# A one-core encoder layer: operands of the MLP's first product made early, parked in device memory and loaded at the borders of token chunks; gate weights split by columns

## The chip, the cores and the metric

The kernel runs on one core of a Trainium2 chip. The metric is the device time of one execution in microseconds (us); for the kernel before it is 1885.21 us, the median of three runs (1883.59 to 1886.38).

## What is computed

One encoder layer over two token groups with shared weights, 512 and 1024 tokens of width 1024, all in float32. Cut to what matters here:

```
h = x + concat(attention, pooling) @ w_out          # attention stage
m = rmsnorm(h, norm_mlp_g)
h = h + square(relu(m @ w_up)) @ w_down             # MLP: 1024 -> 4096 -> 1024
gate = sigmoid(rmsnorm(h, norm_ple_g) @ w_ple_gate)
h = h + gate * (p @ w_ple_proj)                     # gate stage
y = rmsnorm(h, final_norm_g)
```

Every matrix operand is kept as a sum of two parts, a rounded high part and the rest as a low part, and a product takes three matmuls (high by high, high by low, low by high).

## The kernel before

**Tiling.** The 1536 tokens are three chunks c of 512 (`CH`). An activation tile is 128 features by 2 blocks of 128 features by 512 tokens: four of them, `hT[c][a]`, make up a chunk's residual `h`. All tiles of any size share one pool of 49 equal slots of on-chip memory (line 76); a load waits until the slot that it was given is released.

**Order of the work.** Four engines (TensorE, ScalarE, VectorE, GpSimd) follow the order in which the program writes their instructions (line 72); the transfers are all issued by SyncE's one queue. `load` (line 55) keeps a load's place in that order behind the last matmul written before it, without a wait on it. Small work that is to be slipped in between is a generator in the list `chores`; `step()` (line 519) advances the first one by one step. In the attention loop `step` is called once in an iteration `at` (some of them only, lines 1046 to 1047), and in the MLP once after every product.

**Attention stage** (to about 580 us): when a chunk's `h` is finished (`heads_out`, line 735), two chores are queued: `mean_square` (line 641), which squares `h`, sums the squares by features on GpSimd, sums over the partitions by a matmul with ones and stores the row in `w_d[c]`, and `spill` (line 700), which stores `h` in device memory.

**MLP stage** (580 to 1683 us): 48 *pairs* of hidden blocks, 16 for each chunk (class `Pair`, line 756). The first product of a pair is done with seven block products instead of eight. Its token operands, `MO[c][i]` for i = 1 to 7, are made by `operands(c)` (line 599) from four copies `m` of the chunk's `h` (`load_m`, line 594): 8 scalings by `norm_mlp_g` (ScalarE), 8 differences (VectorE), 14 high parts (ScalarE) and 14 low parts (GpSimd and VectorE in turn); each operand is two slots of 128 x 4 x 256. The weights' side is made by `feed` (line 774), some four products ahead.

`run` (line 831) writes a pair in this order, where P means one of the seven products (12 matmuls of 256 columns) and D(a) the second product of the pair before, for one tile of `h` (`down`, 12 matmuls of 512 columns): P1, D(0), P6, P2, D(1), P5, P7, D(2), P3, P4, D(3). `after(i)` comes behind each product and holds the weights' feed, a quarter of the split of the second product's weights, in a chunk's last pair the steps of the next chunk's `operands`, and a `step()`. P3 goes on in the PSUM bank of P5 and waits until VectorE has made `u4` of it (line 858); D(0) waits for the two `r` (line 878).

The MLP runs on unscaled `h`: at a chunk's first pair (g = 0) `raise_h(c)` (line 661) multiplies the four tiles of `h` by the stored row (VectorE), and after the chunk the row is inverted (`invert`, line 667) and multiplied in (`lower_h`), and `stat_g` gets the gate's norm; these are chores of the next chunk's pairs, and for the last chunk of the gate stage. Their loads (`load_h`, `load_ms`) are written at the top of the pair.

*Border 1* is the change from attention to the MLP: the last pieces of `fill`, then `operands(0)` and the mean squares as chores, four steps of the weights' feed, then pair 0 (lines 1060 to 1070; pair 0 has no D). *Borders 2 and 3* are the changes of chunk at pairs 16 and 32. *Border 4* is the change to the gate stage (lines 1171 to 1182): the weights of the two gate products are loaded by rows (`load_g`, `load_p`), scaled by `norm_ple_g` and split (`split_g`), and `gate_in` makes the token operands of chunk 0; all of this is queued before the last four D and stepped through there.

**Gate stage** (from 1683 us): `gate` (line 1187) does one block of 128 output features: `pj`, 6 matmuls, then `pg`, 24 matmuls over the eight row blocks k of the gate weights.

## Time and profile before

| what | value |
|---|---|
| median of three runs | 1885.21 us (1883.59 to 1886.38) |
| the profiled execution: its own time / its span | 1887.41 us / 1885.6 us |
| mean granted TensorE clock, share of full speed | 0.970 |
| TensorE busy | 1772.4 us, 94% of the span |
| weight loads / VectorE / ScalarE / GpSimd busy | 82% / 66% / 50% / 54% |
| moved by DMA | 203.60 MB, 31.1% of the DMA engines' time |

Times in the rows are microseconds from the start of the span. PE is TensorE's matmuls, DVE VectorE, ACT ScalarE, POOL GpSimd, SPq SyncE's queue. A row of a timeline gives the start, the duration, the engine, the line, the operation with output and inputs, how many were joined into the row, and in brackets the idle time ahead of it with what ended it. Line 49 is the helper through which every matmul goes, so PE rows are told apart by their tiles: px, py, pz and pq are the banks of the first product (px: P1 and P2, py: P6, pz: P5 and P3, pq: P7 and P4), pd is the second product, w the ones-matmul of a mean square, pj and pg the gate's.

### The profile page before, as it was taken

What the parts mean: (1) busy time and instruction counts of PE and PEld (TensorE: products, weight loads), DVE (VectorE), ACT (ScalarE), POOL (GpSimd) and SP (SyncE); (2) the same over time, 40 slices, a digit from 0 to 9 for tenths busy, and PEclk for the clock granted to TensorE, in tenths of its full rate; (3) what the DMA queues carried; (4) which work ended last, traced back from release to release, by engine and by line L of the source; (5) the groups of instructions that cost most, each with busy time, mean ns of one, the idle gap of its engine ahead of it and who ended that gap; (6) DMA issues with size and microseconds to landing.
All of it is one profiled execution on the core that took longest, in us unless ns stands there. A gap on an engine that the chain in (4) does not pass through costs nothing.

```text
span 1885.6 us, 28256 instructions
## 1 busy us (share of the span) xinstructions
PE 1772.4 (94%) x10540; PEld 1552.4 (82%) x10540; DVE 1246.7 (66%) x1829; ACT 937.7 (50%) x1830; POOL 1013.9 (54%) x888
## 2 busy tenths in 40 slices
PE   9999899999994799999969999998899999979997
PEld 7888777988873789989958899987788899968897
DVE  5677856888874656555587855556786655573765
ACT  6344456677864444454545544455455444451332
POOL 4475765455545565566556665565556665561122
PEclk9999999999996899999979999999899999999998
DMA  6333453010212433232433423242333332240102
GB/s 238 112 135 146 173 205 135 24 57 29 90 73 99 158 101 101 90 109 95 133 109 119 142 90 112 90 136 87 125 134 105 105 104 90 93 165 12 62 34 101
DMA packets 59929, 203.60 MB, mean 108 GB/s; under 512 B 7568, under 2 KB 10000, under 8 KB 59792
## 3 DMA queue, kind: packets, MB, share of 16 engines
q1 hardware_dynamic: 59792, 201.80, 31.1%
q8 instruction: 83, 1.36, 0.3%
q14 instruction: 54, 0.44, 0.1%
HBM read 169.53 MB, written 32.24 MB: 107 GB/s over the span
## 4 chain that ended last, share of the span: by engine, by line
PE 56%; DVE 5%; ACT 2%; issue 2%; POOL 1%; DMA 0%; POOLq 0%; DVEq 0%; SPq 0%; ACTq 0%
PE pd L49 26%; PE pz L49 7%; PE pq L49 7%; PE px L49 6%; PE pg L49 5%; PE py L49 3%; PE pj L49 1%; DVE h L1241 1%; DVE r L878 1%; DVE wg L1085 1%; DVE h L829 1%; DVE wd L809 0%; DVE mo L626 0%; DMA w<-w_d 0%; DVE h L675 0%
## 5 line engine op out<-in xcount | busy, mean ns | idle before, releaser
L49 PE MATMUL pd<-r,wd 128*128 128x512 f32 x2304 | 571.8, 397 | 19.3 <-DVE r L878 19.3
L49 PEld LDWEIGHTS pd<-r,wd 128*128 128x128 f32 x2304 | 422.7, 190 | 108.0 <-DVE r L878 23.9
L779 POOL TENSOR_TENSOR w<-ws,w 128x512 fp32r<-128x512 f32 x192 | 273.7, 1430 | 235.3 <-ACT w L778 226.4
L829 DVE TENSOR_TENSOR h<-pd,h 128x1024 f32<-128x1024 f32 x192 | 234.4, 1221 | 112.1 <-PE pd L49 112.1
L779 POOL TENSOR_TENSOR w<-wur,w 128x512 fp32r<-128x512 f32 x144 | 212.3, 1487 | 177.0 <-ACT w L778 175.3
L778 ACT CAST w<-ws 128x512 fp32r<-128x512 f32 x192 | 118.6, 618 | 245.4 <-DVE ws L787 214.3
L461 POOL TENSOR_SCALAR pr<-pr,rr 128x512 f32<-128x512 f32 x160 | 111.1, 705 | 145.0 <-DVE rr L456 73.2
L49 PEld LDWEIGHTS pz<-mo,w 128*128 128x128 f32 x1152 | 153.3, 193 | 30.2 <-issue 22.0
L49 PE MATMUL pz<-mo,w 128*128 128x256 f32 x1152 | 156.5, 286 | 21.0 <-DVE u L858 21.0
L49 PE MATMUL z<-w,x 128*128 128x512 f32 (+1 forms) x864 | 175.1, 359 | 1.2 <-DVE w L160 0.5
L49 PEld LDWEIGHTS z<-w,x 128*128 128x128 f32 x864 | 142.4, 188 | 28.2 <-ACT w L159 2.1
L809 DVE TENSOR_TENSOR wd<-wdr,wd 128x512 fp32r<-128x512 f32 x96 | 99.5, 1036 | 98.1 <-ACT wd L808 91.7
L49 PE MATMUL pq<-mo,w 128*128 128x256 f32 x1152 | 155.4, 285 | 1.8 <-DVE c L862 1.6
L49 PE MATMUL px<-mo,w 128*128 128x256 f32 x1152 | 153.5, 283 | 0.0
L49 PE MATMUL pg<-hg,wg 128*128 128x512 f32 (+1 forms) x768 | 142.6, 341 | 11.1 <-DVE h L829 11.1
L49 PEld LDWEIGHTS px<-mo,w 128*128 128x128 f32 x1152 | 148.1, 191 | 4.2
L49 PEld LDWEIGHTS pq<-mo,w 128*128 128x128 f32 x1152 | 146.2, 193 | 2.6 <-issue 2.5
L49 PEld LDWEIGHTS pg<-hg,wg 128*128 128x128 f32 x768 | 120.7, 191 | 28.9 <-issue 11.5
L472 ACT CAST pt<-tp 128x512 fp32r<-128x512 f32 x160 | 87.9, 592 | 91.9 <-PE tp L53 90.1
L809 POOL TENSOR_TENSOR wd<-wdr,wd 128x512 fp32r<-128x512 f32 x96 | 127.2, 1325 | 6.0 <-ACT wd L808 6.0
L473 DVE TENSOR_TENSOR pt<-tp,pt 128x512 fp32r<-128x512 f32 x160 | 104.1, 684 | 33.1 <-ACT pt L472 32.9
L878 DVE TENSOR_TENSOR r<-c,r 128x512 fp32r<-128x512 f32 x96 | 77.7, 815 | 70.1 <-ACT c L875 56.1
(192 smaller groups left out, 2979.5 us busy)
## 6 DMA issues: line engine op xcount, KB each, us to landing
wur<-in_w_up_dram SPq DMA_DIRECT2D x96, 512.0 KB, 3.8
wdr<-in_w_down_dram SPq DMA_DIRECT2D x96, 512.0 KB, 3.7
h_d<-h SPq DMA_DIRECT2D x16, 512.0 KB, 2.8
h<-h_d SPq DMA_DIRECT2D x16, 512.0 KB, 5.8
xn<-in_xn_dram SPq DMA_DIRECT2D x12, 512.0 KB, 6.2
qs_d<-qs SPq DMA_DIRECT2D x12, 512.0 KB, 3.0
yT_d<-y SPq DMA_DIRECT2D x12, 512.0 KB, 2.9
qb<-qs_d SPq DMA_DIRECT2D x12, 512.0 KB, 4.3
```

The source lines that it names most:

```text
L49: last_pe[0] = nc.tensor.matmul(*a, **k).ins
L461: gp.tensor_scalar(p, p, rr, 1.0, op0=ALU.mult, op1=ALU.mult)
L472: sc.copy(self.pt[kt][:, 0], tp)
L473: ve.tensor_tensor(self.pt[kt][:, 1], tp, as32(self.pt[kt][:, 0]), op=ALU.subtract)
L778: sc.copy(t[:, 0], x)
L779: gp.tensor_tensor(t[:, 1], x, as32(t[:, 0]), op=ALU.subtract)
L809: (gp, ve)[i].tensor_tensor(lo, self.dr[i][:, h], as32(hi), op=ALU.subtract)
L829: ve.tensor_tensor(h, pd.rearrange("p (a b) -> p a b", a=2), h, op=ALU.add)
L878: ve.tensor_tensor(self.r[i][:, 1], x, as32(self.r[i][:, 0]), op=ALU.subtract)
L1085: ve.scalar_tensor_tensor(WG[k][1], raw, g, as32(WG[k][0]), op0=ALU.mult, op1=ALU.subtract)
L1241: ve.scalar_tensor_tensor(h, h, gfin_sb[:, 2 * a + e:2 * a + e + 1], r, op0=ALU.mult, op1=ALU.mult)
```

## The change

- `mean_square`, `load_m` and `operands` are replaced by one chore, `make_m(c, et, el)`. For each half b of the blocks it loads two tiles of the stored `h`, squares them and adds the squares, scales them, forms the four differences on engine `et` and the seven operands' halves, the high part on ScalarE and the low part on engine `el`, and stores each half operand in device memory (`mo_d`); at the end comes the mean-square row. For chunk 0 it is queued in the attention stage with GpSimd for both engines, and there the operands are loaded back at once (`load_mo`). For chunks 1 and 2 it is queued at pair g = 1 of the chunk before, with VectorE and GpSimd, and `load_mo(c + 1, i)` is written behind product i of the chunk's last pair. The attention loop steps the chores in every iteration above 54.
- `raise_h` is no longer a chore: one tile follows each product of the chunk's first pair except product 6. The loop that emptied the chores at g = 0 is gone. `invert(c)` is done in the chunk itself at g = 1 and the inverse is stored.
- At border 1 the feed's four steps go between the last pieces of `fill`, and nothing else is run before pair 0 but the steps that these pieces take along.
- Gate weights are loaded in pieces of 512 rows by 256 columns and split by output block d, two blocks ahead of their use, without the scaling. `gate_in` now scales by `norm_ple_g`; for chunk 0 it is done during chunk 1 (`put_in`), stored, and loaded in the last pair; for chunks 1 and 2 it is done in the last block of the chunk before. The first weights (`first_weights`) are loaded and split from the last pair on.
- In `rsqrt_rows` the PSUM bank `bc` is taken later.

```diff
@@ rsqrt_rows: bc taken behind dg and the wait @@
-        bc = tp_ps(f"bc{name}")
...
+            bc = tp_ps(f"bc{name}")
...
+        bc = tp_ps(f"bc{name}")
@@ load_m, operands and mean_square go; make_m and load_mo come @@
-    def load_m(c):
...
-    def operands(c):
...
-    def mean_square(c, e=ve):
...
+    def make_m(c, et, el):
         A, B = slice(0, HF), slice(HF, CH)
+        acc = slot([P, 2, CH], F32, f"sqm{c}")
+        def squares_of(b, m):
+            for i in range(2):
+                sq = slot([P, 2, CH], F32, f"sqm{c}{b}{i}")
+                for h in range(2):
+                    out = sq[:, h] if b + i + h else acc[:, 0]
+                    yield ((lambda i=i, h=h, out=out: sc.activation(out, m[i][:, h], AF.Square)),
+                           (lambda out=out, first=b + i + h == 0: None if first else
+                            et.tensor_tensor(acc[:, 0], acc[:, 0], out, op=ALU.add)))
+        for b in range(2):
+            m = [slot([P, 2, CH], F32, f"m{c}_{2 * i + b}") for i in range(2)]
+            for i in range(2):
+                load(m[i], h_d[c][2 * i + b])
+            yield
+            yield from lagged(squares_of(b, m))
+            for i in range(2):
+                for h in range(2):
+                    k = 2 * (2 * i + b) + h
+                    sc.activation(m[i][:, h], m[i][:, h], AF.Copy, scale=gmlp_sb[:, k:k + 1])
+                yield
+            tt = [slot([P, 2, 2, HF], F32, f"t{c}_{b}{i}") for i in range(2)]
+            t1, t2, t3, t4 = (tt[i // 2][:, i % 2] for i in range(4))
+            b11, b12, b21, b22 = m[0][:, :, A], m[0][:, :, B], m[1][:, :, A], m[1][:, :, B]
+            for o, x, y in ((t1, b12, b11), (t2, b22, t1), (t3, b22, b12), (t4, b21, t2)):
+                et.tensor_tensor(o, x, y, op=ALU.subtract)
+                yield
+            def pairs():
+                for i, x in ((1, b11), (6, t2), (2, b21), (5, t1), (7, t3), (3, b22), (4, t4)):
+                    out = slot([P, 2, 2, HF], F32R, f"mm{c}_{i}{b}")
+                    def low_part(i=i, x=x, out=out):
+                        el.tensor_tensor(out[:, 1], x, as32(out[:, 0]), op=ALU.subtract)
+                        for j in range(2):
+                            sy.dma_start(mo_d[c][i][j][:, 2 * b:2 * b + 2], as32(out[:, j]))
+                        if c == 0 and b:
+                            load_mo(0, i)
+                    yield (lambda x=x, out=out: sc.copy(out[:, 0], x)), low_part
+            yield from lagged(pairs())
         sh = slot([P, 2, CH], F32R, f"sh{c}")
         sc.copy(sh[:, 0], acc[:, 0])
+        el.tensor_tensor(sh[:, 1], acc[:, 0], as32(sh[:, 0]), op=ALU.subtract)
+        yield from wait(2)
         bc = tp_ps(f"w{c}")
         for i in range(2):
             pe.matmul(bc, ones_sb, sh[:, i], start=i == 0, stop=i == 1)
+        ve.tensor_scalar(acc[:, 1], bc, 1.0 / D, EPS, op0=ALU.mult, op1=ALU.add)
+        sy.dma_start(w_d[c], acc[:, 1])
+    def load_mo(c, i):
+        MO[c, i] = [slot([P, 4, HF], F32R, f"mo{c}_{i}{j}") for j in range(2)]
+        for j in range(2):
+            load(as32(MO[c, i][j]), mo_d[c][i][j])
@@ invert @@
             ve.reciprocal(w, w)
             yield
+        sy.dma_start(w_d[c], ws[c])
@@ heads_out, a chunk's last piece @@
-                    chores.extend((mean_square(c, gp), spill(c)))
+                    chores.append(spill(c))
+                    if c == 0:
+                        chores.append(make_m(0, gp, gp))
@@ the attention loop @@
-        if at == 96:
-            load_m(0)
-        if at == 97:
+        if at == 94:
...
-            if took or at < 84 and at % 2:
+            if took or at > 54 or at % 2:
@@ border 1 @@
-    made = operands(0)
-    made = [act for i in (0, 1, 6, 2, 5, 7, 3, 4) for act in made[i]]
-    chores.append(steps_of(*[lambda i=i: [act() for act in made[i:i + 2]] for i in range(0, len(made), 2)]))
     while fill:
         fill.popleft()()
         step(2)
-    for _ in range(4):
-        next(feeding)
-        step(2)
-    while chores:
-        step()
+        if len(fill) % 2 == 0 and len(fill) < 8:
+            next(feeding)
@@ gate weights and operands @@
-    def load_g(k):
...
-    def split_g(k):
...
+    def load_g(q, j):
+        WG["r", q, j] = slot([P, 4, 2 * P], F32, f"wgr{q}{j}")
+        load(WG["r", q, j], w_gate[j * CH:(j + 1) * CH, q * 2 * P:(q + 1) * 2 * P].rearrange("(k p) d -> p k d", p=P))
+    def split_g(d, e):
+        if d not in WG:
+            WG[d] = [slot([P, KD, P], F32R, f"wg{d}_{i}") for i in range(2)]
+        for j in range(2):
+            raw = WG["r", d // 2, j][:, :, d % 2 * P:(d % 2 + 1) * P]
+            hi, lo = (x[:, 4 * j:4 * j + 4] for x in WG[d])
+            sc.copy(hi, raw)
+            yield
+            e.tensor_tensor(lo, raw, as32(hi), op=ALU.subtract)
+            yield
...
-    def gate_in(c, e, n=4):
...
+    def gate_in(c, a):
+        hl = [slot([P, 2, CH], F32R, f"hg{c}{a}_{i}") for i in range(2)]
+        for h in range(2):
+            g = gple_sb[:, 2 * a + h:2 * a + h + 1]
+            sc.activation(hl[0][:, h], hT[c][a][:, h], AF.Copy, scale=g)
+            ve.scalar_tensor_tensor(hl[1][:, h], hT[c][a][:, h], g, as32(hl[0][:, h]), op0=ALU.mult, op1=ALU.subtract)
+        gin[c, a] = hl
...
+    def put_in(c):
+        for a in range(4):
+            gate_in(c, a)
+            for i in range(2):
+                sy.dma_start(hg_d[a][i], flat(gin[c, a][i]))
+            del gin[c, a]
+            yield
+    hg_d = [[dram.tile([P, D], F32, name=f"hg_d{a}{i}") for i in range(2)] for a in range(4)]
+    def load_in(c, a):
+        gin[c, a] = [slot([P, 2, CH], F32R, f"hg{c}{a}_{i}") for i in range(2)]
+        for i in range(2):
+            load(flat(gin[c, a][i]), hg_d[a][i])
+    def first_weights():
+        for j in range(2):
+            load_g(0, j)
+        load_p(0), load_p(1), load_pp(0)
+        yield
+        for d in range(2):
+            yield from split_g(d, (gp, ve)[d])
+        split_p(0)
+        yield
+        split_p(1)
+        yield
+        split_pp(0, ve)
@@ the pairs @@
+        raising = None
         if g == 0:
             for a in range(4):
                 load_h(c, a, h_d[c][a])
             load_ms(c)
-            chores.append(raise_h(c))
-        if g == 1 and c:
-            load_ms(c - 1)
-        if g == NG - 1 and c < 2:
-            made = operands(c + 1)
-        if g == NG - 2 and c < 2:
-            load_m(c + 1)
-        if pair is last_pair:
-            load_p(0), load_p(1), load_g(0)
-            for a in range(4):
-                load_h(0, a, hl_d[0][a])
-        elif n == 0:
+            raising = raise_h(c)
+        if g == 1:
+            chores.append(invert(c))
+            if c:
+                load_ms(c - 1)
+                chores.extend((lower_h(c - 1, ve), stat_g(c - 1, ve), store_h(c - 1)))
+            if c == 1:
+                chores.append(put_in(0))
+            if c < 2:
+                chores.append(make_m(c + 1, ve, gp))
+        if n == 0:
             pair.load_down()
         splits = pair.split_down()
...
         def after(i):
             next(feeding, None)
             next(splits, None)
-            if i == 1:
-                for act in made.get(0, ()):
-                    act()
-            for act in made.get(i, ()):
-                act()
+            if raising and i != 6:
+                next(raising, None)
+            if g == NG - 1 and c < 2:
+                load_mo(c + 1, i)
+            if n == len(pairs) - 1:
+                if i == 1:
+                    chores.append(first_weights())
+                if i in (5, 7, 3, 4):
+                    load_in(0, (5, 7, 3, 4).index(i))
             step()
         pair.run(between, after)
         for _ in splits:
             pass
-        if g == 0:
-            while chores:
-                step()
-        if g == 1 and c:
-            chores.extend((invert(c - 1), lower_h(c - 1, ve), stat_g(c - 1, ve), store_h(c - 1)))
+        for _ in raising or ():
+            pass
         before = pair
-    chores.append(steps_of(lambda: split_p(0), lambda: split_p(1), lambda: split_g(0)))
-    for k in range(1, KD):
-        load_g(k)
-    load_pp(0)
-    late = gate_in(0, gp)
-    chores.append(steps_of(*[lambda: next(late) for _ in range(5)], *[lambda k=k: split_g(k) for k in range(1, KD)]))
+    for a in range(4):
+        load_h(0, a, hl_d[0][a])
     for a in range(4):
         before.down(a)
-        step(4)
+        step(2)
@@ gate @@
+        if c == 0 and d % 2 == 0 and d < KD - 2:
+            for j in range(2):
+                load_g(d // 2 + 1, j)
+        splits = split_g(d + 2, (gp, ve)[d % 2]) if c == 0 and d < KD - 2 else iter(())
         for k in range(KD):
-            ws = [x[:, cols] for x in WG[k]]
-            for i, (w_, x_) in enumerate(three(ws, [x[:, k % 2, tok] for x in gin[c, "h"][k // 2]])):
+            ws = [x[:, k, :] for x in WG[d]]
+            for i, (w_, x_) in enumerate(three(ws, [x[:, k % 2, tok] for x in gin[c, k // 2]])):
                 pe.matmul(pg, w_, x_, start=k == 0 and i == 0, stop=k == KD - 1 and i == 2)
             if k in hooks:
                 step()
+            if k % 2 == 0:
+                next(splits, None)
+            elif c < 2 and d == KD - 1:
+                del gin[c, k // 2]
+                gate_in(c + 1, k // 2)
@@ the groups of the gate stage @@
+            if c == 0 and d == 0:
+                load_ms(2)
+                chores.extend((lower_h(2, ve), stat_g(2, ve)))
             if d == 4 and c < 2:
                 load_pp(c + 1)
-                coming.append(gate_in(c + 1, ve))
+            if c == 0 and d == 4:
+                for a in range(4):
+                    load_h(1, a, hl_d[1][a])
+            if c < 2 and d == KD - 1:
+                split_pp(c + 1, ve)
             gate(c, o, w, d, sq)
-            if c == 1 and d in (5, 6):
-                next(coming[-1])
-        if c == 0:
-            load_ms(2)
-            for a in range(4):
-                load_h(1, a, hl_d[1][a])
-            chores.extend((invert(2), lower_h(2, ve), stat_g(2, ve)))
         chores.append(finish(c, o, w, sq))
     while chores:
         step()
```

## Rows read from the trace of the kernel before

**Rows 1.** Which engine is busy when: from the page, TensorE's busy share and its granted clock in 40 equal slices of 47.1 us, in tenths.

```profile
PE   9999899999994799999969999998899999979997
...
PEclk9999999999996899999979999999899999999998
```

**Rows 2.** TensorE's waits over the whole span: tile and line that waited, what ended the wait; us in total, times, longest us.

```profile
PE w L49 <- ACT sh L647: 26.3, 1, 26.3
PE pz L49 <- DVE u L858: 21.0, 3, 8.1
PE pd L49 <- DVE r L878: 19.3, 5, 8.8
PE pg L49 <- DVE h L829: 11.1, 1, 11.1
```

**Rows 3.** TensorE's timeline at border 1.

```profile
577.93 1.69 PE L49 MATMUL po<-cat,wo 128*128 128x256 f32 x12 [0.28 <-DVE h L749]
...
607.82 2.76 PE L49 MATMUL px<-mo,w 128*128 128x256 f32 x12
...
625.20 2.90 PE L49 MATMUL pz<-mo,w 128*128 128x256 f32 x12 [8.05 <-DVE u L858]
...
654.99 1.58 PE L49 MATMUL px<-mo,w 128*128 128x256 f32 x12
```

**Rows 4.** TensorE's timeline at border 2: P1 of pair 15, the wait in D(0) of pair 16, P1 of pair 17.

```profile
929.26 1.57 PE L49 MATMUL px<-mo,w 128*128 128x256 f32 x12
...
969.78 5.08 PE L49 MATMUL pd<-r,wd 128*128 128x512 f32 x11 [8.02 <-DVE r L878]
...
991.61 1.57 PE L49 MATMUL px<-mo,w 128*128 128x256 f32 x12
```

**Rows 5.** TensorE's timeline at border 3: P1 of pair 31, P1 and the D(0) behind it of pair 33, P1 of pair 34.

```profile
1289.18 1.57 PE L49 MATMUL px<-mo,w 128*128 128x256 f32 x12
...
1352.46 1.59 PE L49 MATMUL px<-mo,w 128*128 128x256 f32 x12
1353.89 3.04 PE L49 MATMUL pd<-r,wd 128*128 128x512 f32 x12
...
1373.64 1.58 PE L49 MATMUL px<-mo,w 128*128 128x256 f32 x12
```

**Rows 6.** TensorE's timeline in the gate stage: pj of the first two blocks, and of two blocks in the steady part.

```profile
1683.03 1.57 PE L49 MATMUL pj<-pp,wpj 128*128 128x512 f32 x6
...
1703.91 1.31 PE L49 MATMUL pj<-pp,wpj 128*128 128x512 f32 x5
...
1710.82 1.56 PE L49 MATMUL pj<-pp,wpj 128*128 128x512 f32 x6
...
1717.76 1.56 PE L49 MATMUL pj<-pp,wpj 128*128 128x512 f32 x6
```

**Rows 7.** SyncE's timeline at border 1: the store of the last chunk's h, then the loads of pair 0.

```profile
573.20 11.87 SPq L702 DMA_DIRECT2D h_d<-h  x4
...
609.20 1.35 SPq L56 DMA_DIRECT2D h<-h_d  x3
610.64 0.38 SPq L56 DMA_DIRECT2D w<-w_d  x1
611.08 2.45 SPq L56 DMA_DIRECT2D wdr<-in_w_down_dram  x4
```

**Rows 8.** VectorE's timeline in pair 0: the first multiplication of h, and u4.

```profile
616.93 1.22 DVE L664 TENSOR_TENSOR h<-h,w 128x1024 f32<-128x1024 f32 x1 [7.58 <-DMA w<-w_d]
...
624.64 0.41 DVE L858 TENSOR_TENSOR u<-pz,u 128x256 f32<-128x256 f32 x1
```

**Rows 9.** Two stretches of 5 us by engine: PE, PEld, DVE, ACT, POOL busy us and count, granted clock, share of the DMA engines, GB/s moved.

```profile
20.00:25.00 5.00, 5.00 (x28) 4.25 (x27) 4.08 (x6) 3.88 (x5) 0.00 (x0) 1.00 1.04 410
...
1660.00:1665.00 5.00, 5.00 (x35) 4.61 (x34) 3.45 (x5) 0.00 (x0) 0.30 (x1) 1.00 0.99 361
```

**Rows 10.** Transfers: count, KB each, median us from issue to landing.

```profile
h<-h_d SPq DMA_DIRECT2D x16, 512.0 KB, 5.8
...
m<-h_d SPq DMA_DIRECT2D x12, 512.0 KB, 5.1
```

**Rows 11.** Groups of instructions by line and shape: busy us in all and mean ns of one, idle before (the first four); and for the tile t of line 617, ns min/median/max.

```profile
L626 POOL TENSOR_TENSOR mo<-t,mo 128x512 fp32r<-128x512 f32 x12 | 17.9, 1488 | 12.0 <-ACT mo L622 12.0
...
L622 ACT CAST mo<-t 128x512 fp32r<-128x512 f32 x24 | 14.0, 617 | 19.4 <-DVE t L617 19.4
...
L160 DVE SCALAR_TENSOR_TENSOR w<-w1r,gmix_sb,w 128x1024 fp32r<-128x1024 f32 x7 | 9.0, 1283 | 5.4 <-ACT w L159 5.4
...
L1085 DVE SCALAR_TENSOR_TENSOR wg<-wgr,gple_sb,wg 128x1024 fp32r<-128x1024 f32 x8 | 19.3, 2456 | 0.0
...
L617 DVE TENSOR_TENSOR t<-m,t x12: 678/680/1744, 574.3 to 1325.5; 128x512 f32<-128x512 f32 x12
```

**Rows 12.** Two stretches of 50 us in the attention stage, columns as in Rows 9.

```profile
400.00:450.00 50.00, 49.50 (x317) 42.77 (x316) 43.12 (x84) 39.81 (x97) 31.98 (x40) 1.00 0.08 28
450.00:500.00 50.00, 50.00 (x322) 43.79 (x321) 42.79 (x86) 38.15 (x94) 21.59 (x32) 1.00 0.25 96
```

**Rows 13.** A weight load on SyncE's queue in pair 13, and ScalarE's first use of it in pair 14.

```profile
894.32 2.58 SPq L56 DMA_DIRECT2D wur<-in_w_up_dram  x2
...
916.71 0.62 ACT L778 CAST w<-wur 128x512 fp32r<-128x512 f32 x1
```

More of the change, by code (lines that the diff above doesn't have):

```diff
@@ L641, in mean_square @@
-    def mean_square(c, e=ve):
-        out = []
-        yield from squares(c, "m", out, e)
-        acc = out[0]
-        yield from wait(1)
+    def make_m(c, et, el):
+        A, B = slice(0, HF), slice(HF, CH)
+        acc = slot([P, 2, CH], F32, f"sqm{c}")
[35 more added lines that the diff above has]
+            yield from lagged(pairs())
@@ L646, in mean_square @@
         sh = slot([P, 2, CH], F32R, f"sh{c}")
         sc.copy(sh[:, 0], acc[:, 0])
-        gp.tensor_tensor(sh[:, 1], acc[:, 0], as32(sh[:, 0]), op=ALU.subtract)
-        yield from wait(3)
+        el.tensor_tensor(sh[:, 1], acc[:, 0], as32(sh[:, 0]), op=ALU.subtract)
+        yield from wait(2)
         bc = tp_ps(f"w{c}")
@@ L681, in stat_g @@
         yield from wait((3, 2, 3)[c])
-        acc = out[0]
-        bc = yield from rsqrt_rows([acc[:, 0]], CH, f"g{c}")
-        sc.copy(acc[:, 1], bc)
-        bcs[c] = acc[:, 1]
+        bc = yield from rsqrt_rows([out.pop()[:, 0]], CH, f"g{c}")
+        if c != 1:
+            bcs["t"] = slot([P, 2, CH], F32, f"bcs{c}")
+        sc.copy(bcs["t"][:, c % 2], bc)
+        bcs[c] = bcs["t"][:, c % 2]
         yield
-    mraw, MO, ws = {}, {}, {}
+    MO, ws = {}, {}
     HF = CH // 2
+    ORDER = (1, 6, 2, 5, 7, 3, 4)
+    mo_d = [{i: [dram.tile([P, 4, HF], F32, name=f"mo_d{c}_{i}{j}") for j in range(2)] for i in ORDER} for c in range(3)]
     def load_pool(c):
@@ L812, in product @@
         def product(self, i, out, fresh=True):
-            w, m = self.w.pop(i), MO[self.c][i]
+            w, m = self.w.pop(i), MO[self.c, i]
             for k in range(4):
@@ L1075, in encoder_layer @@
     WG, WP, gin = {}, {}, {}
-    def load_g(k):
-        WG[k] = slot([P, D], F32, f"wgr{k}")
-        load(WG[k], w_gate[k * P:(k + 1) * P, :])
-    def split_g(k):
-        raw, WG[k] = WG[k], [slot([P, D], F32R, f"wg{k}_{i}") for i in range(2)]
-        g = gple_sb[:, k:k + 1]
-        sc.activation(WG[k][0], raw, AF.Copy, scale=g)
-        ve.scalar_tensor_tensor(WG[k][1], raw, g, as32(WG[k][0]), op0=ALU.mult, op1=ALU.subtract)
+    def load_g(q, j):
[11 more added lines that the diff above has]
+            yield
     def load_p(k):
@@ L1125, in encoder_layer @@
         c, g = pair.c, pair.g
-        made = {}
+        raising = None
         if g == 0:
@@ L1207, in gate @@
                 step()
-        if d == KD - 1 and c < 2 and o == 0:
-            for _ in coming.pop():
-                pass
         s = slot([P, w], F32, f"s{c}{o}{d}")
```

56 lines of the change are left out of this document (5 added, 51 removed).

## The prediction

> **What bounds the kernel.** I looked first at which engine is busy when. TensorE is at nine tenths or more in nearly every slice, and the dips in its busy share and its granted clock lie together in slices 13 and 14, 21, 28 and 36 [rows 1]. So the kernel is bound by TensorE, but for a few places. TensorE's waits name them: 26.3 us once on a mean square, 21.0 us in three waits on `u4`, 19.3 us on `r`, 11.1 us ahead of the first gate product [rows 2]; the timelines show that the long ones stand at the four borders. The tile named as what ended the last of these is not the cause: it was VectorE's queue, full of gate weights.
>
> A wait is not yet the loss, since the clock falls with it and matmuls behind it run slower. So I measure each border by the work that it holds at full clock. A pair takes 1373.64 - 1352.46 = 21.2 us undisturbed, a product 1353.89 - 1352.46 = 1.43 us [rows 5].
> - Border 1: from the end of the last `po`, 577.93 + 1.69 = 579.6, to P1 of pair 2 at 654.99 are 75.4 us [rows 3]. In it are pair 0 without D (7 x 1.43 = 10.0) and pair 1 (21.2): lost **44.2**.
> - Border 2: P1 of pair 15 to P1 of pair 17 is 991.61 - 929.26 = 62.4 [rows 4], less two pairs: lost **20.0**.
> - Border 3: likewise 1352.46 - 1289.18 = 63.3 [rows 5]: lost **20.9**.
> - Border 4: the first gate block takes 1703.91 - 1683.03 = 20.9, a later one 1717.76 - 1710.82 = 6.9 [rows 6]: lost **14.0**.
>
> Together 99 us, 5% of the time, and this is all that the change can win.
>
> **The change, part by part.** *Border 1.* Operands and mean square of chunk 0 are ready in the attention stage, those of chunks 1 and 2 no longer run here, so P1 can start at 579.6. Next in the way is `h`. The last store of `h_d` waits for the last sum into `h`, and only behind it on SyncE's queue come the loads of `h`, of the row and of the second product's weights. In the trace that store ended at 573.20 + 11.87 = 585.1, because VectorE was late with operands; without them I put it at 580.2. From the issue of the `h` loads at 609.20 [rows 7] to P3, which waits for `u4`, it was 625.20 - 609.20 = 16.0 us [rows 3, 7]: `h` and the row landed and the first multiplication began at 616.93, `u4` came at 624.64 [rows 8]. The new order of VectorE is the same here: one multiplication behind P1, another before `u4`, and a split of the late weights between them. With one `h` load more in the queue, some 1.5 us (512 KB at the 361 GB/s of [rows 9]), P3 starts at 580.2 + 16.0 + 1.5 = 597.7, and P1 of pair 2 comes 654.99 - 625.20 = 29.8 us behind P3 as now, at 627.5. **Gain 27.5**, 16.7 stay. Bounds: 22 (store no earlier than now) and 44 (loads overtake the store).
>
> *Borders 2 and 3.* `operands` leaves the last pair: 22 ScalarE, 22 VectorE and GpSimd instructions, which the two long waits were made of. What comes instead is transfers: 14 loads of 512 KB in the last pair, 7.3 MB, beside 2.1 MB of weights, then 2.1 MB of `h` and 0.26 MB of row, all on one queue. The fullest stretches moved 361 to 410 GB/s [rows 9]. If each operand load waits for the slot that product i gives back, they are written from 1.4 to 18.3 us of the pair, and at 390 GB/s the row lands some 13 us into the next pair. VectorE stands there in the first multiplication; behind it wait D(0)'s sum into `h`, hence the PSUM bank that D(2) needs at 12.7 us, and `u4`, which P3 needs at 15.5 us. Written out in VectorE's order this holds TensorE 2.9 us at D(2), 1.7 at P3, 1.9 at P4 and 1 at the next D(0): **7.5 us stay, gain 12.5 and 13.4**. Bounds for each: 0 (the row so late that the old wait returns) and 20 (the queue runs ahead of the program and everything is in time).
>
> The page "DMA: Bandwidth & Descriptors" of the Trainium skill, section on where the 436 GB/s come from, says that a transfer between device memory and on-chip memory is held to about 358 GB/s. The trace agrees in one stretch and not in the other, 361 and 410 [rows 9]. By 358 alone the 11.8 MB would end about 3 us later than at 390, an estimate from the page's figure, and each border would keep some 10 us.
>
> *Border 4.* The gate's weights and token operands come split and in time: 17 transfers of 512 KB from the start of the last pair on, 8.9 MB, 25 us at 361 GB/s against 32 us of matmuls. The splits up to the first block need ten ScalarE halves at 0.62 and six GpSimd halves at 1.49 us [rows 11], in 14 steps under the same matmuls. One us stays for the PSUM banks. **Gain 13** (8 to 14).
>
> *What is added in the attention stage.* `make_m(0)`, 31 ScalarE instructions at 0.62 and 30 GpSimd ones at 1.49 us [rows 11], minus the mean square that was there, 9 and 8 of them: some 14 and 33 us more, spread over about 40 iterations or 140 us. TensorE is full there, ScalarE busy 38 to 40 of 50 us, GpSimd 22 to 32 [rows 12]. Both have room, but ScalarE stands in the chain from scores to products. **Cost 2**; bounds 0 and 33 (all of GpSimd's new work on the path).
>
> *In the chunks.* `make_m(1)` and `make_m(2)` add the same counts over six pairs each, 127 us in which ScalarE and GpSimd have about half their time free (the table of busy shares); TensorE's matmuls are the cover, and without it the 19 us of ScalarE would show. New waits: ScalarE stands twice per chunk for the `m` loads, 5.1 us to landing [rows 10] against 1.4 to 4.2 us between steps. Behind it are `t` of P1 and the relus. **Cost 2** for both chunks; bounds 0 and 4 x 5.1 = 20. SyncE's 28 stores of half operands each wait for GpSimd and hold weight loads behind them. The load issued at 894.32 is first used at 916.71 [rows 13], 22 us later; pinned to its place in the program, 18.3 us into pair 13 that began at 929.26 - 42.4 = 886.9 [rows 4], it would be issued at 905.2 and still land 7 us early. Cost 0.
>
> The contention of VectorE and GpSimd could be feared here: the same difference takes 678 ns alone and up to 1744 [rows 11]. The page "SBUF — State Buffer", section "Who interferes with whom", of the Trainium skill says that a VectorE instruction with two on-chip inputs waits out a GpSimd instruction that reads on-chip memory. That agrees with these rows; by it all 15 such instructions of a chunk would take 26 us instead of 10.
>
> Neither is put on the path: TensorE's waits on VectorE are eight in all, and the long ones of them stand at borders [rows 2].
>
> *Gate stage.* For chunks 1 and 2, `gate_in` with scaling moves into the last block: eight two-input VectorE instructions of half 1283 ns (0.64) to half 2456 ns (1.23) [rows 11], 5.1 to 9.8 us, in step with 13.9 us of matmuls that take them one tile at a time. **Cost 2** for both, bounds 0 and 20.
>
> Sum: 27.5 + 12.5 + 13.4 + 13 - 6 = **60 us**. The profiled execution took 1887.4, 1.8 beyond its span and 2.2 above the median of the runs, so 1827 there and **1825** by the median.
>
> **Rivals.** *All borders go clean* (0.20). For it: SyncE now runs up to 11 us ahead of the program [rows 13], and at a chunk's end no `m` and `t` fill the slots. Against it: 11.8 MB in one queue. Gain 99 - 6 = 93, 1792.
> *The row and `h` come so late that borders 2 and 3 win nothing* (0.13). For it: in border 1 VectorE stood 7.58 us for this very row [rows 8]. Gain 27.5 + 13 - 6 = 34, 1851.
> *Chunk 0's operands aren't ready* (0.04), that is the change doesn't do what it says: `make_m(0)` needs about 40 steps and has hardly more iterations. Then border 1 keeps another 15 to 20 us: 1843.
> *Slower* (0.06): the weights come late in each of the 12 pairs that carry `make_m`, since every store on SyncE's queue stands for GpSimd. It decides from about 5 us a pair (60 / 12), that is from SyncE falling 12 us behind its place; at 8 us a pair it is 96 - 60, 1921. Against it: 7 us to spare, worked out above.
> *As forecast* (0.55). The 0.02 left lie between this case and the slower one, at no change.
>
> **Numbers.** Point 1825. The range takes in the clean case at its lower end and the case of borders 2 and 3 at its upper one, with the bounds of the added work between them: 1790 to 1855. Faster by over 0.2% (4 us, about what a measurement of this kernel can tell): 0.92; within 0.2%: 0.02; slower: 0.06.
>
> **What would show it.** Right: `w` by `sh` gone from TensorE's waits; P1 of pair 0 within 2 us of the last `po`; P3 of pair 0 still waiting for `u4` some 11 us; at pairs 16 and 32 several waits under 4 us each, with the DMA share near 1; the second gate block 7 to 8 us behind the first; VectorE's multiplications of `h` beginning 10 to 15 us into the pair. Wrong: an operand load ending a wait of TensorE at P1 or P6, ScalarE's first square of `m` holding P2, `po` waiting for VectorE or GpSimd in the attention stage, or pairs 2 to 8 of a chunk over 21.2 us.

## The result and the profile after

The changed kernel takes **1875.79 us** (median of four runs, 1874.47 to 1876.62), the kernel before 1885.33 beside it: ratio 0.995, 95% interval 0.9932 to 0.9967. It is faster by some 10 us; forecast were 60, and the range (1790 to 1855) does not hold the time. The profiled execution took 1874.47 us with a span of 1872.7. Of all runs below, two profiled executions were slow (1953 us in experiment one, 3322 us in the kernel with three edits together), so both are left out of the medians and only waits are read from the trace of the first.

TensorE's busy share and granted clock of the kernel after, in 40 slices of 46.8 us, answer to [rows 1]:

```profile
PE   9999899999969798999999998999999999999997
...
PEclk9999999999989899999999999999999999999998
```

The dips at the borders (slices 14, 21, 28, 36 of [rows 1]) have shrunk or are gone, but slice 12 (515 to 562 us), in the attention stage, has a six that was not there. TensorE's waits over the span (tile and line that waited, what ended the wait; us in total, times, longest) answer to [rows 2]:

```profile
PE pz L49 <- issue: 14.2, 3, 13.1
PE pd L49 <- DVE r L883: 12.2, 11, 3.7
PE S L49 <- ACT pr L449: 10.3, 2, 6.7
PE w L49 <- POOL sh L643: 6.8, 2, 3.7
PE pq L49 <- DVE c L867: 4.8, 1, 4.8
PE pz L49 <- DVE u L863: 4.7, 1, 4.7
```

The 26.3 us on the mean square and the 11.1 ahead of the first gate product have left the list. New in it are waits that belong to no border: S in the attention stage, and w, pq, pz in the middle of chunks. The last `po`, then P1 of pairs 0, 2, 15, 17, 31, 33 and 47, from TensorE's timeline of the kernel after, give the accounting; the first rows answer to [rows 3], the later ones to [rows 4, 5]:

```profile
595.73 1.69 PE L49 MATMUL po<-cat,wo 128*128 128x256 f32 x13
597.26 1.57 PE L49 MATMUL px<-mo,w 128*128 128x256 f32 x12
...
617.67 2.90 PE L49 MATMUL pz<-mo,w 128*128 128x256 f32 x12 [13.15 <-issue]
...
647.88 1.60 PE L49 MATMUL px<-mo,w 128*128 128x256 f32 x12
...
935.39 1.58 PE L49 MATMUL px<-mo,w 128*128 128x256 f32 x12
...
980.05 1.58 PE L49 MATMUL px<-mo,w 128*128 128x256 f32 x12
...
1306.94 1.59 PE L49 MATMUL px<-mo,w 128*128 128x256 f32 x12
...
1351.62 1.58 PE L49 MATMUL px<-mo,w 128*128 128x256 f32 x12
...
1651.87 1.33 PE L49 MATMUL px<-mo,w 128*128 128x256 f32 x10
```

| stretch | before, us | after, us | forecast | measured |
|---|---|---|---|---|
| start to the end of the last `po` (after: to P1 of pair 0, right behind it) | 579.6 | 597.3 | +2 | **+17.6** |
| border 1: from there to P1 of pair 2 | 75.4 | 50.6 | -27.5 | -24.8 |
| pairs 2 to 14 | 274.3 | 287.5 | +1 | **+13.2** |
| border 2: P1 of pair 15 to P1 of pair 17 | 62.4 | 44.7 | -12.5 | -17.7 |
| pairs 17 to 30 | 297.6 | 326.9 | +1 | **+29.3** |
| border 3: P1 of pair 31 to P1 of pair 33 | 63.3 | 44.7 | -13.4 | -18.6 |
| pairs 33 to 46 | 298.3 | 300.3 | 0 | +2.0 |
| P1 of pair 47 to the end (border 4, gate) | 234.9 | 220.8 | -11 | -14.1 |

The right column sums to -13.1; the spans differ by 1885.6 - 1872.7 = 12.9. So the four rows with borders gave back 75 us, more than the 64 forecast for them. The other four lost 62 us to the work that was moved under matmuls, where the forecast had 4.

**Where the 62 us stand in the trace.** First the attention stage, ScalarE's timeline of the kernel after (in brackets the idle time ahead and what ended it), then SyncE's and TensorE's over the same stretch:

```profile
529.65 0.69 ACT L449 ACTIVATE pr<-S,nm 128x512 f32<-128x512 f32 x1 [3.89 <-DMA mo_d<-mm]
...
538.12 1.07 ACT L472 CAST pt<-tp 128x512 fp32r<-128x512 f32 x2 [3.46 <-DMA mo_d<-mm]
...
546.66 0.69 ACT L449 ACTIVATE pr<-S,nm 128x512 f32<-128x512 f32 x1 [6.64 <-DMA mo_d<-mm]
```

```profile
536.78 1.57 SPq L56 DMA_DIRECT2D mo<-mo_d  x3
538.44 2.16 SPq L636 DMA_DIRECT2D mo_d<-mm  x3
545.33 2.04 SPq L56 DMA_DIRECT2D mo<-mo_d  x3
```

```profile
548.15 2.08 PE L49 MATMUL S<-ks,qb 128*128 128x512 f32 x4 [6.69 <-ACT pr L449]
```

SyncE's queue takes stores of half operands (`mo_d<-mm`) and loads of whole operands (`mo<-mo_d`) in turn. A load reads what a store just ahead of it wrote, so the queue stands some 5 us between them (from 540.60 to 545.33). SyncE's waits from 505 to 556 us (what waited, for what; us in total, times, longest) have this first:

```profile
SPq L56 <- DMA mo_d<-mm: 24.8, 12, 6.1
```

The stores behind go out late, their slots stay taken, and ScalarE, which wants such a slot for the next `pr` or `pt`, stands in the chain from scores to products. TensorE runs dry at S (3.64 and 6.69 us) and once behind `pt` (2.12).

Second, pair 4, SyncE's, ScalarE's and TensorE's timelines:

```profile
695.58 8.28 SPq L636 DMA_DIRECT2D mo_d<-mm  x5
703.95 1.52 SPq L56 DMA_DIRECT2D m<-h_d  x2
```

```profile
708.18 0.63 ACT L607 ACTIVATE sqm<-m 128x512 f32<-128x512 f32 x1 [8.99 <-DMA m<-h_d]
```

```profile
712.29 2.90 PE L49 MATMUL pq<-mo,w 128*128 128x256 f32 x12 [4.79 <-DVE c L867]
```

The load of the second two `m` stands behind five stores that wait for GpSimd's low parts, and is issued 8.4 us after the first of them. ScalarE has reached the first square of `m` and waits 9 us; behind it are the splits of the weights, VectorE behind those, and P4's bank behind VectorE. Pair 4 takes 27.84 us instead of 21.1. Pair 23 is the same (7.51 us on ScalarE, 28.74 us), pair 21 in part (3.72 just ahead of it, 25.92).

Third, pair 20, VectorE's timeline and TensorE's:

```profile
1049.02 1.91 DVE L1115 SCALAR_TENSOR_TENSOR hg<-h,gple_sb,hg 128x512 fp32r<-128x512 f32 x2 [3.40 <-ACT hg L1114]
1050.86 3.44 DVE L883 TENSOR_TENSOR r<-c,r 128x512 fp32r<-128x512 f32 x2
```

```profile
1052.66 0.96 PE L49 MATMUL pd<-r,wd 128*128 128x512 f32 x3 [3.67 <-DVE r L883]
```

`put_in`, which makes chunk 0's gate operands, writes two ScalarE scalings and, right behind, two VectorE instructions that need them. VectorE stands 3.40 us for ScalarE, with the two `r` of the pair queued behind; D(0) waits for them, and the pair takes 28.74 us. Fourth, pairs 7 and 25: the ones-matmul of the mean-square row waits for GpSimd's low part of it, and the pair takes 26.99 and 27.80 us.

```profile
766.13 0.50 PE L49 MATMUL w<-sh,ones_sb 128*128 128x512 f32 x1 [3.66 <-POOL sh L643]
```

Against the same pairs of the kernel before, pairs 4 and 7 are 6.7 + 5.8 = 12.5 us longer, of the 13.2; pairs 17, 18, 20, 21, 23 and 25 are 1.5 + 0.8 + 6.3 + 4.8 + 7.8 + 6.9 = 28.1 us longer, of the 29.3.

### The profile page after: what moved, and what is told of

Same layout as the page of the kernel before. It is cut to its first block, busy times and chain, and to the rows that moved or that the text cites. A ratio compares the mean times of both kernels' runs of the same rounds, so it can differ in the third digit from the quotient of the medians.

```text
span 1872.7 us, 28563 instructions
## 1 busy us (share of the span) xinstructions
PE 1779.1 (95%) x10540; PEld 1551.8 (83%) x10540; DVE 1248.2 (67%) x1831; ACT 940.8 (50%) x1854; POOL 1030.5 (55%) x909
## 4 chain that ended last, share of the span: by engine, by line
PE 47%; DVE 5%; ACT 3%; POOL 3%; issue 2%; DMA 2%; POOLq 0%; DVEq 0%; SPq 0%; ACTq 0%
PE pd L49 21%; PE pg L49 6%; PE px L49 5%; PE pz L49 5%; PE pq L49 5%; PE py L49 3%; PE pj L49 1%; POOL mm L634 1%; POOL w L784 1%; DVE h L834 1%; DVE r L883 1%; ACT w L783 1%; DMA w<-w_d 1%; DVE wd L814 1%; POOL wd L814 0%
## 5 line engine op out<-in xcount | busy, mean ns | idle before, releaser
L461 POOL TENSOR_SCALAR pr<-pr,rr 128x512 f32<-128x512 f32 x160 | 111.1, 705 | 143.9 <-DVE rr L456 63.3
L814 DVE TENSOR_TENSOR wd<-wdr,wd 128x512 fp32r<-128x512 f32 x96 | 105.6, 1100 | 109.0 <-ACT wd L813 89.9
L813 ACT CAST wd<-wdr 128x512 fp32r<-128x512 f32 x192 | 118.8, 619 | 13.5 <-DMA wdr<-in_w_down_dram 11.5
```

Source lines behind the costliest of these rows:

```text
L461: gp.tensor_scalar(p, p, rr, 1.0, op0=ALU.mult, op1=ALU.mult)
L813: sc.copy(hi, self.dr[i][:, h])
L814: (gp, ve)[i].tensor_tensor(lo, self.dr[i][:, h], as32(hi), op=ALU.subtract)
```

## The experiments

Four causes are proposed, each with its own edit; the rival each time is that the added work itself fills the engines, so that the delay stays or moves to another place. Times are medians of four runs, of three in experiment one and in the kernel with three edits; ratios are to the kernel before, run on the same chip (1885.4 to 1886.7 us there).

**One: the first square of `m` four steps further behind its load.** The load keeps its place in the queue.

```diff
                 load(m[i], h_d[c][2 * i + b])
-            yield
+            yield from wait(5 if c else 1)
```

> One edit to the changed kernel: for chunks 1 and 2 the chore that makes the operands waits five steps instead of one between its load of the stored h and the first square. Theory of the waits: ScalarE stood 9.0, 3.7 and 7.5 us for these loads in pairs 4, 20 and 23, and everything queued behind it made pairs 4, 21 and 23 last 27.8, 25.9 and 28.7 us; with the load landed first, they come back to 21 to 22 us and the time falls by 15 to 19 us, to about 1859. Rival, the added work itself fills ScalarE, VectorE and GpSimd: the long pairs move by two or stay as long, and the time stays within 4 us of 1876.

Measured: 1857.21 us, ratio 0.9845 (0.9828 to 0.9861), 18.6 below the changed kernel. The group of ScalarE's squares of `m` (busy us, mean ns; idle time ahead of it) of the kernel after, and of this one:

```profile
L607 ACT ACTIVATE sqm<-m 128x512 f32<-128x512 f32 x24 | 15.2, 634 | 24.5 <-DMA m<-h_d 16.9 <-issue 7.5
```

```profile
L607 ACT ACTIVATE sqm<-m 128x512 f32<-128x512 f32 x24 | 15.2, 632 | 2.3 <-DMA m<-h_d 2.3
```

Of ScalarE's 24.5 us of waits 2.3 are left, and no work was taken away: these loads were issued too close to their use. The edit also moves the rest of each chore back, by four steps for each half; what that did is told behind the experiment on border 1.

**Two: the mean-square row's matmul four steps later.**

```diff
         el.tensor_tensor(sh[:, 1], acc[:, 0], as32(sh[:, 0]), op=ALU.subtract)
-        yield from wait(2)
+        yield from wait(6 if c else 2)
```

> One edit to the changed kernel: for chunks 1 and 2 the ones-matmul of the mean square is written six steps instead of two behind the GpSimd subtraction that it reads. Theory of the waits: TensorE stood 3.7 and 3.2 us in it in pairs 7 and 25 and ran the next matmuls at a lower clock; pairs 7 and 25 go from 27.0 and 27.8 us to 21.5, and the time falls by 10 to 13 us, to about 1865. Rival, GpSimd is so far behind that its late results hold TensorE elsewhere: another wait of 3 us or more on a GpSimd result appears in the next pairs and the time stays within 4 us of 1876.

Measured: 1875.37 us, ratio 0.9945 (0.9923 to 0.9966), no gain. Its VectorE and TensorE timelines in pair 7:

```profile
765.12 0.69 DVE L798 TENSOR_TENSOR ws<-wur,wur 128x512 f32<-128x512 f32 x1 [3.25 <-DMA mo_d<-mm]
765.73 3.45 DVE L883 TENSOR_TENSOR r<-c,r 128x512 fp32r<-128x512 f32 x2
```

```profile
767.54 5.47 PE L49 MATMUL pd<-r,wd 128*128 128x512 f32 x11 [2.43 <-DVE r L883]
```

The wait on `sh` is gone from this place and another stands there. VectorE waits 3.25 us for a slot whose content is still being stored, and D(0) for the `r` behind it; the pair takes 27.35 us. This wait of VectorE was in the kernel after too, hidden behind the one on `sh`:

```profile
762.58 0.69 DVE L798 TENSOR_TENSOR ws<-wur,wur 128x512 f32<-128x512 f32 x1 [3.19 <-DMA mo_d<-mm]
```

So the row was no cause of its own. The time is as the rival had it, the new wait is not the one that it named (on a GpSimd result). Its root may be the same: those stores wait for GpSimd's low parts, and GpSimd was busy from 741.4 to 773.2 us with one gap of 0.16. That the late stores are the cause is read from the trace; no run here shows it.

**Three: chunk 0's operands loaded back only when all are stored.**

```diff
-                        if c == 0 and b:
-                            load_mo(0, i)
...
         sy.dma_start(w_d[c], acc[:, 1])
+        for i in ORDER if c == 0 else ():
+            yield
+            load_mo(0, i)
```

> One edit to the changed kernel: chunk 0's operands are loaded back one by one after all of them have been stored, instead of each right behind its store. Theory of the waits: SyncE's queue stands in each load for its own store to land, the next stores come late, and the slots that ScalarE's exponentials are to write are held by them (3.9, 3.5 and 6.6 us of ScalarE in 526 to 547 us); without it P1 of pair 0 begins at 582 to 585 us instead of 597.3, and the time falls by 11 to 15 us unless the later loads hold P1. Rival, the 14 us of ScalarE and 33 us of GpSimd added to a full attention stage are what makes it longer: P1 of pair 0 stays after 593 and the time within 4 us of 1876.

Measured: 1858.61 us, ratio 0.9851 (0.9836 to 0.9867), 17.2 below the changed kernel. SyncE's timeline, and TensorE's at P1 of pair 0:

```profile
509.33 27.11 SPq L636 DMA_DIRECT2D mo_d<-mm  x14
...
543.66 11.63 SPq L56 DMA_DIRECT2D mo<-mo_d  x12
```

```profile
583.50 1.56 PE L49 MATMUL px<-mo,w 128*128 128x256 f32 x12
```

Fourteen stores run through without a load between them, and P1 of pair 0 starts at 583.50 instead of 597.26. ScalarE has no wait on `mo_d<-mm` left from 500 to 590 us. So 13.8 of the 17.6 us came with the loads back; 3.9 are left for the added instructions (2 to 6 in the kernels further on, whose P1 comes between 581.6 and 585.5). The edit changes two things at once: the queue no longer stands behind its own stores, and the fourteen slots of the loaded operands are taken later. Their shares were not told apart.

**Four: `put_in` in two steps**, ScalarE's half of a tile in one, VectorE's in the next.

```diff
         for a in range(4):
-            gate_in(c, a)
+            ...
+            for h in range(2):
+                sc.activation(hl[0][:, h], hT[c][a][:, h], AF.Copy, scale=gs[h])
+            yield
+            for h in range(2):
+                ve.scalar_tensor_tensor(hl[1][:, h], ...)
+            yield
```

> One edit to the changed kernel: the chore that makes chunk 0's gate operands writes ScalarE's half in one step and VectorE's half in the next. Theory of the waits: in pair 20 VectorE stood 3.4 us for ScalarE's half with the subtraction that makes r behind it, TensorE waited 3.7 and 0.7 us for r and the pair took 28.7 us; in two steps pair 20 takes 21 to 23 us and the time falls by 5 to 7 us. Rival, VectorE's and ScalarE's added work is what fills the pair: pair 20 and the one behind it together stay as long as now, 54.7 us, and the time within 3 us of 1876.

Measured: 1865.77 us, ratio 0.9887 (0.9872 to 0.9902), 10.0 below the changed kernel. Pair 20 takes 21.10 us instead of 28.74. The gain is more than was expected, and not all of it is the wait. The eight added steps move every chore behind them; pairs 17 to 30 take 316.6 instead of 326.9 us, and what is left stands elsewhere: a wait for `m` in pair 24 (26.45), the row's matmul on `sh` in pair 27 (28.14, a wait of 3.52).

**One, three and four together, then two more.**

> The three edits that helped alone, together: m loads five steps ahead of their use for chunks 1 and 2, chunk 0's operands loaded back after all stores, chunk 0's gate operands in two steps. Theory of the waits: P1 of pair 0 begins by 585 us, pairs 4 and 20 to 24 take 21 to 23 us each, the pairs that hold the chores' ends (one in chunk 0, one or two in chunk 1) stay at 26 to 28; the time is 1834 to 1842, the single gains of 19, 18 and 11 us less what they share in chunk 1. Rival, the chores' work itself fills the engines: the delay moves to other pairs and the time stays above 1850.

Measured: 1828.97 us, ratio 0.9697 (0.968 to 0.9713), lower than expected. The single gains are 18.6 + 17.2 + 10.0 = 45.8, together they give 46.8: the three edits act on separate delays.

The fifth edit keeps the last three half operands' slots from being given out again for a while:

```diff
+        held = deque(maxlen=3)
...
                     out = slot([P, 2, 2, HF], F32R, f"mm{c}_{i}{b}")
+                    if c:
+                        held.append(out)
```

> As the run with the three edits, and in chunks 1 and 2 the program keeps the last three half operands before their slots are given to others. Theory of the slots: in the pair that holds the end of a chore VectorE stood 3.3 us for a slot whose half operand was still being stored, the subtraction for r came late and the pair took 27 to 28 us; with later reuse this wait goes, these pairs take 22 to 24 us and the time falls by 6 to 12 us against that run. Rival, in these pairs r is late because VectorE and GpSimd hold each other up (the two subtractions took 3.45 us instead of 1.4): the pairs stay at 26 to 28 us and the time within 4 us of that run.

Measured: 1829.08 us, ratio 0.9692 (0.9676 to 0.9708): no gain. Both sides expected pairs of 26 to 28 us to start from, but with edit one the pairs at issue were already short: in the next kernel, which does not hold the slots, they are 22.5 to 24.8 us. So this run does not test whether the late stores made pairs 7 and 25 long.

**Border 1.** The 13.15 us ahead of P3 are the largest wait left. The loads of `h` and its row, moved ahead of the last stores of `h` (with one, three and four, and without the fifth):

```diff
         fill.popleft()()
         step(2)
+        if len(fill) == 5:
+            for a in range(4):
+                load_h(0, a, h_d[0][a])
+            load_ms(0)
```

> As the run with the three edits, and chunk 0's h and its row are loaded when five pieces are left in the attention stage instead of at the top of pair 0. What the prediction put at border 1: TensorE waits 13 us in pair 0 for u4 because the loads of h stand behind the last store of h and two weight loads. If so the wait goes down to 3 us or less, the pair takes 14 to 17 us instead of 27.6, and the time falls by 9 to 13 us. Rival, the wait ends with the split of the second product's weights, which is loaded as late as before: it stays at 8 us or more and the time falls by less than 5.

Measured: 1828.04 us, ratio 0.969 (0.9675 to 0.9704), 0.9 below the three edits, as the rival had it. The wait is 11.85 us; VectorE's first multiplication came early, at 588.40, but P3 was not waiting for it alone. ScalarE's timeline of this kernel and TensorE's:

```profile
595.88 0.62 ACT L814 CAST wd<-wdr 128x512 fp32r<-128x512 f32 x1 [10.15 <-DMA wdr<-in_w_down_dram]
```

```profile
602.26 2.90 PE L49 MATMUL pz<-mo,w 128*128 128x256 f32 x12 [11.85 <-issue]
```

ScalarE stands for the second product's weights, which sit behind the same stores; VectorE's half of that split stands ahead of `u4`.

This trace also shows where edit one acts. In chunk 0, behind border 1, this kernel differs from the one of experiment three by edit one alone: pairs 4 and 5 take 43.5 us instead of 49.7, pairs 6 to 8 take 64.9 instead of 69.7. So 6.2 us of its gain there are the wait for `m`, and 4.9 are the delay at the end of the chore that edit two did not remove. Why that delay went with the later steps was not separated.

All five edits together:

> The three edits, later reuse of the half operands' slots, and h loaded before border 1, together. Theory of the waits: the gains add, and the time is 1812 to 1826. Rival, as the slots run short with all of them, loads wait for slots elsewhere and the time is no lower than the better one of the two runs with four edits, less 2 us.

Measured: 1825.37 us, ratio 0.9681 (0.9666 to 0.9695), in the range at its upper end and 0.7 below the rival's bound, so it decides little between them. Then both loads ahead of the stores, and the weights alone:

```diff
+        if len(fill) == 5:
+            pairs[0].load_down()
...
-        if n == 0:
-            pair.load_down()
```

> All five edits, and the loads of pair 0's second-product weights moved ahead of the last three stores of h, beside the loads of h. Theory: what is left at border 1 is a chain of two loads, each behind the last stores of h on SyncE's queue; with h alone early the wait ahead of pair 0's P3 was 11.75 us, ended by the split of these weights on ScalarE at 594.24. With both early nothing is behind the stores: the wait falls to 0 to 3 us, and the time from 1825.4 to 1814 to 1818. Rival, the time goes elsewhere: the six loads hold the stores of h or the next up weights back, or P4 and the first second product wait instead: the wait at P3 falls but the time stays within 4 us of 1825.

> As the kernel with all five edits, but h and its row loaded where the changed kernel loads them, and only the second-product weights of pair 0 loaded ahead of the last stores of h. Theory of two loads in parallel: VectorE's first multiplication begins as late as with nothing early, 598.4 (11 us behind its predecessor), and the wait at P3 falls only from 13.3 to 9 to 11 us; time 1824 to 1828. Rival, the weights alone hold the border: the wait falls to 3 us or less, and the time to 1816 to 1820.

Measured: both, 1818.56 us, ratio **0.9646** (0.9627 to 0.9665); weights alone, 1820.43, ratio 0.9659 (0.9642 to 0.9677). The waits ahead of P3 in the kernel with both, and in the one with the weights alone:

```profile
596.41 2.90 PE L49 MATMUL pz<-mo,w 128*128 128x256 f32 x12 [4.55 <-ACT w L787]
```

```profile
598.30 2.90 PE L49 MATMUL pz<-mo,w 128*128 128x256 f32 x12 [8.97 <-issue]
```

The wait falls as two parallel loads would have it: 13.3 with neither early (the run with the fifth edit), 11.8 with `h`, 9.0 with the weights, 4.6 with both. That is more than the 0 to 3 expected: ScalarE stood 5.29 us for the next up weights, a third transfer behind the stores, and VectorE's `u4` came no sooner, at 595.89. The time follows less neatly: with both, P1 of pair 0 itself came at 584.61, 3.0 us later than with `h` alone early (581.63), and the time ended 0.6 us above what was expected. With the weights alone the time came 3.6 us below the range expected, near the rival's 1820, though the wait was not the rival's; the two spans are equal (1818.0 and 1818.3). Why P1 moved by some 3 us between kernels whose attention work is the same, is not settled; there is one trace of each.

## Why the prediction was wrong

That the kernel gets faster was right; 60 us were forecast and 10 came. **The failed steps** are the two costs of moved work. *What is added in the attention stage*, put at 2, measured 17.6; *In the chunks*, put at 2 for both chunks, measured 42.5 with `put_in` in it. The same error is in both: I priced the added instructions against the free time of ScalarE and GpSimd, and not the order of SyncE's queue. With the order mended the price was near in the attention stage (3.9 us) and in chunk 0 (2.4 us left in pairs 2 to 14 of the first kernel with a border-1 edit), but not in chunk 1, where 9.6 us are left in pairs 17 to 30, unexplained.

- *"SyncE's 28 stores of half operands each wait for GpSimd and hold weight loads behind them ... Cost 0."* The mechanism was named, and looked for at the wrong load. The weights had 22 us in hand [rows 13]. The loads of `m` are used one step behind their issue and had none. Experiment one: 18.6 us, in chunk 0 somewhat more than half of it this wait.
- *"ScalarE stands twice per chunk for the `m` loads, 5.1 us to landing"*. The place was right, the price was not: 5.1 is from issue to landing [rows 10], but the wait of 8.99 us began at 708.18 - 8.99 = 699.19, 4.8 us before the load was issued. So the bound 4 x 5.1 = 20 was not one: the wait of 8.99 and the 7.51 of pair 23 go past its 5.1, and that pairs 4, 21 and 23 together lost 19.3, inside 20, is luck.
- *The attention stage* was bounded by GpSimd's work (0 to 33). What came was neither: a load behind its own store, in a queue whose other stores hold the slots that ScalarE needs. The rows of before show no such pair of transfers, and I did not ask when a slot comes back. Experiment three: 17.2 us, 13.8 of them ahead of P1 of pair 0. That 17.6 lies within 0 to 33 says nothing for the bound.
- *`put_in` in chunk 1* is not in the sum at all. I counted that the gate's token operands are loaded in the last pair, and left out where they are made. Experiment four: 10.0 us, 7.6 of them in pair 20.
- *"Neither is put on the path"*, said of VectorE and GpSimd holding each other up. Pairs 7 and 25, at the ends of the chores, lost 12.7 us with `sh`, `r` and stores late behind a full GpSimd; in pair 7 two subtractions for `r` took 3.44 us. Edit two shows that the row alone was not it; what was, stays open.

**Steps that held.** *Border 1*: 24.8 against 27.5. P1 follows the last `po` at once, and P3 waits 13.15 us where 11 were forecast. The reason given, `h` and its row behind the last store, was half of it: with these early the wait fell only to 11.85, since the second product's weights stand in the same place. *Borders 2 and 3*: 17.7 and 18.6 against 12.5 and 13.4. The "several waits under 4 us" are seen at border 2 in the four places forecast (D(2), P3, P4 and the next D(0)), but none is over 1.1:

```profile
969.52 3.06 PE L49 MATMUL pd<-r,wd 128*128 128x512 f32 x12 [0.19 <-DVE h L834]
973.10 1.66 PE L49 MATMUL pz<-mo,w 128*128 128x256 f32 x12 [0.52 <-issue]
975.77 1.66 PE L49 MATMUL pq<-mo,w 128*128 128x256 f32 x12 [1.01 <-issue]
...
983.79 1.42 PE L49 MATMUL pd<-r,wd 128*128 128x512 f32 x5 [0.89 <-DVE r L883]
```

44.66 less two pairs of 21.2 leaves 2.3 us, not 7.5. The queue was faster than the 390 GB/s that I took, and VectorE's first multiplication of `h` began at 966.40, 9.9 us into the pair, instead of some 13. Stretches of the kernel after around border 2, with the columns of [rows 9]:

```profile
945.00:950.00 5.00, 5.00 (x35) 4.59 (x34) 4.22 (x7) 0.58 (x2) 1.61 (x1) 1.00 1.03 415
950.00:956.50 6.50, 6.50 (x42) 5.81 (x41) 3.28 (x5) 3.56 (x8) 2.52 (x2) 1.00 1.03 410
956.50:962.00 5.50, 5.50 (x37) 4.97 (x36) 2.43 (x3) 3.62 (x7) 4.45 (x5) 1.00 1.02 408
```

The page "DMA: Bandwidth & Descriptors" of the Trainium skill, section "Where 436 GB/s comes from", says that about 358 GB/s, a core's half of what its memory gives, binds such transfers. These 17 us of operand, weight and `h` loads moved 408 to 415, so by the measurement that limit did not bind in this kernel, which runs on one core.

*Border 4*: 14.1 against 13 with 2 taken off for the gate stage. The second block starts 7.10 us behind the first, where it was 20.9 [rows 6], and no cost shows:

```profile
1684.64 1.55 PE L49 MATMUL pj<-pp,wpj 128*128 128x512 f32 x6
...
1691.74 1.54 PE L49 MATMUL pj<-pp,wpj 128*128 128x512 f32 x6
```

**The rivals.** Clean borders (0.20) were nearly what happened at borders 2 to 4. The slower one (0.06) had the right queue and the wrong load, so its condition, 12 us of lag behind the weights' place, was never needed. What the forecast gave for "wrong" (ScalarE's first square of `m`, `po` waiting in the attention stage, pairs over 21.2 us) is what the trace shows, with P4 held in place of P2 and mostly S in place of `po` (one `po`, at 474.88, waited 2.78 us for VectorE). The range failed because bounds that were only worked out for engines (33 and 20) were hardly used: the forecast took 2 of each, and 1855 left room for 30 us in all, and neither bound holds `put_in`.

## What to carry to other kernels

Work that is moved under a busy engine is priced in two parts: its instructions against the free time of its engines, and the place of every transfer it issues in the queue it shares. For each load ask what stands ahead of it in its queue and what that waits for; here a load issued one step before its use, behind stores that wait on an engine, cost their wait, and loads behind their own stores cost the stores' landing (24.8 us of standing) to everything queued after. When a store keeps a buffer taken, find who asks for that buffer next: here it was ScalarE in the scores and VectorE ahead of `r`.

## What was not expected of the hardware

A wait in the middle of full work cost more than its length, since matmuls behind it ran at a lower granted clock. In pair 4 TensorE waited 4.79 us and lost 6.7; stretches ahead of the wait, in it, behind it and after (columns of [rows 9]) show it:

```profile
700.00:707.50 7.50, 7.50 (x50) 6.69 (x49) 4.33 (x4) 0.00 (x0) 4.76 (x4) 1.00 0.52 182
707.50:712.30 4.80, 0.01 (x2) 0.04 (x1) 2.43 (x4) 2.19 (x4) 1.26 (x1) 0.99 0.79 321
712.30:718.00 5.70, 5.70 (x24) 5.15 (x25) 4.33 (x8) 4.19 (x8) 2.06 (x2) 0.71 0.54 184
718.00:724.00 6.00, 6.00 (x39) 5.29 (x39) 5.23 (x6) 5.94 (x12) 3.71 (x4) 1.00 0.41 100
```

Behind the wait the granted clock is 0.71 as a mean over 5.7 us, between its two levels of 1.2 and 2.4 GHz (0.50, the lower one, over the first 2.9 us), and the product after it takes 2.90 us instead of 1.58. The prediction said that the clock falls with a wait at borders, and measured borders by it; the waits that it allowed for inside the chunks it counted at their bare length.
